# Softmax scaling of two heads in four moved from VectorE to GpSimd in a hybrid attention kernel

## The chip, the cores and the metric

The kernel runs on one core of a Trainium2 chip. The metric is device time in microseconds; lower is better. A difference is judged against the spread of the runs of the kernel before.

## What is computed

One layer of width 1024 on 512 tokens: a gated feed-forward block (inner width 2816), an attention mixer, a second feed-forward block and a final norm. In the mixer, eight heads use three branches side by side (compressed keys, selected blocks, and a window as long as the sequence) and eight heads use a window of 128 with a sink. For 512 tokens and eight blocks the selection takes all blocks, so the selected branch is plain causal attention. What matters here:

```python
s = jnp.where(mask, s + bias, NEG_INF)
p = jax.nn.softmax(s, axis=-1)
o = jnp.einsum('bngrqk,bnkgd->bnqgrd', p, vw)
...
g = jax.nn.sigmoid(gate_logits)
return g[..., 0:1] * o_cmp + g[..., 1:2] * o_slc + g[..., 2:3] * o_win
```

## The kernel before, in words

Everything is float32, and each large product is done as three matmuls of split halves (helper `mm3_steps`, L207 to L209: weight high by activation high, by activation low, weight low by activation high). The weight halves are made on the chip: ScalarE rounds (L97), VectorE subtracts (L98).

The mixer works in stages. A stage is one block of 128 queries (index i, 0 to 3), one group g of four heads, and one branch. There are eight stages of class `Swa` (the 128 window) and then fourteen of class `Nsa`: br 1 (selected) and br 2 (window, with the compressed branch beside it) for i = 1, 2, 3, and br 0 (both together) for i = 0. A row of probabilities is 128 or 256 wide in `Swa`, and 256, 384 or 512 wide in `Nsa` for i = 1, 2, 3.

`scores()` of a stage does for each of four heads r: the score matmuls (L838, L839) and the bias matmul (L918), a row maximum on VectorE (L911, in `Swa` L1037), an exponential on ScalarE with the row sum accumulated (L912, in `Swa` L1049). Then come the gate and the reciprocal (L973, L974; in `Swa` L1052, L1053), and each head's probabilities, a tile `tmp`, are multiplied in place by the resulting column of `su`: this is the line of the change, L985 with head 2 on ScalarE at L983, and L1055 in `Swa`. In stages of br 0, L979 does it, which the change doesn't touch.

`outputs()` of a stage then transposes the four heads' probabilities on TensorE, key block by key block (`transposed`, L847, four transposes into one PSUM bank, head 0 first), splits the result (ScalarE L849, VectorE L850) and multiplies by the values (L884, L885). `put_o` copies and splits the result (L855, L860, L866, L867).

`attend` lines the stages up: three heads of scores of a stage, then in turn a step of the outputs of the stage before and a head of scores. Between these steps it puts pieces of other work, the fillers, worked off in a fixed list: projections, the compression network, and the output projection (L1077 adds its result). The code writes down an order of the work; the order of instructions on each engine is made from it when the kernel is built. There is no DMA issued from GpSimd; all are on SP's queue.

Of the kernel before, what the change touches and what calls it, by code (L numbers as in the profile page):

```python
# [13 lines left out]
ALU = mybir.AluOpType  # L14
# [30 lines left out]
def tile_hybrid(ctx, tc, xT, f1_wi, f1_wo, wm_t, wm_n, cw1, cw2, small, wm_oa, wm_ob, wm_oc, f2_wi, f2_wo, const, out):  # L45
    nc = tc.nc
    V, A, PE = nc.vector, nc.scalar, nc.tensor
# [7 lines left out]
    def ps(tag="mm"):  # L55
        return psp.tile([P, 512], F32, tag=tag, name=tag, bufs=NB[tag])
# [17 lines left out]
    def tmp():  # L74
        return sb.tile([P, 512], F32, tag="tmp", name="tmp", bufs=NTMP)
# [563 lines left out]
    def slopes(g):  # L639
        if state["slopes"][0] == g:  # L640
            return state["slopes"][1]
        a = tabs[:, 512:1024].rearrange("p (r k) -> p r k", r=4)
        b = tabs2[:, 0:256].bitcast(BF16).rearrange("p (r k) -> p r k", r=4)
        for r in range(4):
            V.tensor_scalar(a[:, r, :], ident, 2.0 ** -(g * 4 + r + 1), None, op0=ALU.mult)
            V.tensor_scalar(b[:, r, :], ident, 2.0 ** -(g * 4 + r + 1), None, op0=ALU.mult)
        state["slopes"] = g, (a, b)
        return a, b
# [187 lines left out]
    def score(o, q, r, i, k1, k2):  # L836
        qs = slice(i * P, (i + 1) * P)
        PE.matmul(o, q[:, r % 2, qs], k1, start=True, stop=False)  # L838
        PE.matmul(o, q[:, r % 2, qs], k2, start=False, stop=False)  # L839

    def small_t(n, name):
        return sb.tile([P, n], F32, tag="st" + name, name=name, bufs=3)
# [46 lines left out]
    class Nsa:  # L889
# [5 lines left out]
        def scores(self):  # L895
# [5 lines left out]
            c0, c1 = ((0, 12), (0, 4), (4, 12))[br]  # L901
            nm, su = small_t(12, "nm"), small_t(12, "su")
# [25 lines left out]
            for r in range(4):  # L928
                q = Q[4 + 2 * g + r // 2]
                o = ps("sc")  # L930
                p = tmp()[:, : 2 * W if br == 0 else W]
# [43 lines left out]
            for r in range(4):  # L975
                p = self.p[r]
                if br == 0:
                    pv = p.rearrange("p (a b) -> p a b", a=2)
                    V.tensor_tensor(  # L979
                        pv, pv, su[:, r : r + 8 : 4].unsqueeze(2).to_broadcast([P, 2, P]), op=ALU.mult  # L980
                    )
                elif r == 2:
                    A.activation(p, p, AF.Copy, scale=su[:, c0 + r : c0 + r + 1])  # L983
                else:
                    V.tensor_scalar(p, p, su[:, c0 + r : c0 + r + 1], None, op0=ALU.mult)  # L985
            if br != 1:
# [25 lines left out]
    class Swa:  # L1012
# [5 lines left out]
        def scores(self):  # L1018
            g, i, W, c0 = self.g, self.i, self.W, self.c0
            sid, sidb = slopes(g)  # L1020
            nm, su, es = small_t(12, "nm"), small_t(12, "su"), small_t(4, "es")
            sink = nsink[:, g * 4 : g * 4 + 4]
            os_ = []
            for pr in range(2):
                bank = ps("sc")
                for rr in range(2):
                    r = pr * 2 + rr
                    o = bank[:, rr * 256 : rr * 256 + W]
                    score(o, Q[9 + 2 * g + pr], r, i, SK[0][:, g, c0 : c0 + W], SK[1][:, g, c0 : c0 + W])
                    if i == 0:  # L1030
                        PE.matmul(o, sidb[:, r, :], diag, start=False, stop=True)
                    else:
                        PE.matmul(o, sid[:, r, :], dist[:, 256:512], start=False, stop=False)
                        PE.matmul(o[:, :P], idb, swm, start=False, stop=True)
                    os_.append(o)
                    yield 0.4
                V.tensor_reduce(  # L1037
                    nm[:, pr * 2 : pr * 2 + 2], bank.rearrange("p (a b) -> p a b", a=2)[:, :, :W],
                    axis=AX.X, op=ALU.max, negate=True,
                )  # L1040
                if pr == 0:
                    V.tensor_tensor(nm[:, 0:2], nm[:, 0:2], sink[:, 0:2], op=ALU.min)
                else:
                    V.tensor_tensor(nm[:, 2:4], nm[:, 2:4], sink[:, 2:4], op=ALU.min)
            V.tensor_tensor(es, nm[:, :4], sink, op=ALU.subtract)
            self.p = []
            for r in range(4):
                a = tmp()[:, :W]
                A.activation(a, os_[r], AF.Exp, bias=nm[:, r : r + 1], accum_out=su[:, r : r + 1])  # L1049
                self.p.append(a)  # L1050
            A.activation(es, es, AF.Exp)
            V.tensor_tensor(su[:, :4], su[:, :4], es, op=ALU.add)  # L1052
            V.reciprocal(su[:, :4], su[:, :4])  # L1053
            for r in range(4):
                V.tensor_scalar(self.p[r], self.p[r], su[:, r : r + 1], None, op0=ALU.mult)  # L1055
            yield 0

        def outputs(self):
# [216 lines left out]
```

## Time and profile before

| | us |
|---|---|
| median of 3 runs | 1015.99 |
| lowest and highest run | 1015.99 and 1016.55 |
| the profiled execution, its own time | 1014.31 |
| its span, first to last instruction | 1012.5 |
| mean granted TensorE clock | 0.988 |

The profile shows one execution. The feed-forward block takes the span up to about 375 us, the mixer's projections reach to 410, the stages run from 410 to about 632, the mixer's last output projection ends near 700, and the second feed-forward block fills the rest. Lines are those of the kernel before; PE is TensorE's matmul, PEld its weight load, DVE VectorE, ACT ScalarE, POOL GpSimd.

### The profile page before, as it was taken

What the parts mean: (1) busy time and instruction counts of PE and PEld (TensorE: products, weight loads), DVE (VectorE), ACT (ScalarE), POOL (GpSimd) and SP (SyncE); (2) the same over time, 40 slices, a digit from 0 to 9 for tenths busy, and PEclk for the clock granted to TensorE, in tenths of its full rate; (3) what the DMA queues carried; (4) which work ended last, traced back from release to release, by engine and by line L of the source; (5) the groups of instructions that cost most, each with busy time, mean ns of one, the idle gap of its engine ahead of it and who ended that gap; (6) DMA issues with size and microseconds to landing.
All of it is one profiled execution on the core that took longest, in us unless ns stands there. A gap on an engine that the chain in (4) does not pass through costs nothing.

```text
span 1012.5 us, 15908 instructions
## 1 busy us (share of the span) xinstructions
PE 982.1 (97%) x6196; PEld 869.0 (86%) x6196; DVE 804.2 (79%) x1466; ACT 509.6 (50%) x1034; POOL 0.2 (0%) x4
## 2 busy tenths in 40 slices
PE   7799999999999999999999999989999999999997
PEld 5589999999999889788777777769999999999996
DVE  5889878788796675787889898788986878879665
ACT  7544434444344355554677675854434445344344
POOL 0000000000000000000000000000000000000000
PEclk9899999999999999999999999989999999999998
DMA  7053233222324303123311111115322323322112
GB/s 294 1 187 111 77 115 123 87 105 73 114 84 140 122 34 113 42 84 99 117 42 45 40 43 63 48 50 172 116 90 98 136 73 106 113 75 95 42 43 84
DMA packets 36508, 93.62 MB, mean 92 GB/s; under 512 B 4432, under 2 KB 8912, under 8 KB 36432
## 3 DMA queue, kind: packets, MB, share of 16 engines
q1 hardware_dynamic: 36432, 92.59, 26.8%
q8 instruction: 49, 0.80, 0.3%
q14 instruction: 27, 0.22, 0.1%
HBM read 88.87 MB, written 2.10 MB: 90 GB/s over the span
## 4 chain that ended last, share of the span: by engine, by line
PE 89%; DVE 6%; ACT 4%; issue 1%; DMA 1%; SPq 0%; DVEq 0%; ACTq 0%
PE mm L306 9%; PE mm L305 9%; PE mm L307 9%; PE sc L209 8%; PE sc L208 8%; PE sc L207 8%; PE mm L207 4%; PE mm L209 4%; PE mm L208 4%; PE sc L306 4%; PE sc L307 4%; PE sc L305 4%; PE mm L847 3%; PE pv L884 2%; PE pv L885 2%; PE mm L703 1%
## 5 line engine op out<-in xcount | busy, mean ns | idle before, releaser
L306 PE MATMUL mm<-u 128*128 128x256 f32 x760 | 214.5, 282 | 0.0
L307 PE MATMUL mm<-u 128*128 128x256 f32 x760 | 214.4, 283 | 0.0
L305 PE MATMUL mm<-u 128*128 128x256 f32 x760 | 214.3, 282 | 0.0
L207 PE MATMUL sc<-u 128*128 128x512 f32 (+1 forms) x400 | 156.5, 391 | 13.0 <-ACT u L97 12.0
L209 PE MATMUL sc<-u 128*128 128x512 f32 (+1 forms) x400 | 155.4, 388 | 0.8 <-DVE u L98 0.8
L208 PE MATMUL sc<-u 128*128 128x512 f32 (+1 forms) x400 | 155.8, 390 | 0.0
L305 PEld LDWEIGHTS mm<-u 128*128 128x128 f32 x760 | 144.5, 190 | 7.2 <-DVE tmp L512 0.5
L306 PEld LDWEIGHTS mm<-u 128*128 128x128 f32 x760 | 144.8, 191 | 5.6
L307 PEld LDWEIGHTS mm<-u 128*128 128x128 f32 x760 | 144.7, 191 | 0.6
L207 PE MATMUL mm<-u 128*128 128x512 f32 (+1 forms) x248 | 100.3, 404 | 4.6 <-ACT u L97 4.6
L209 PE MATMUL mm<-u 128*128 128x512 f32 (+1 forms) x248 | 96.6, 389 | 0.8 <-DVE u L98 0.8
L208 PE MATMUL mm<-u 128*128 128x512 f32 (+1 forms) x248 | 95.7, 386 | 0.6 <-DVE u L163 0.6
L207 PEld LDWEIGHTS sc<-u 128*128 128x128 f32 x400 | 77.3, 193 | 21.0 <-ACT u L97 12.9
L209 PEld LDWEIGHTS sc<-u 128*128 128x128 f32 x400 | 76.4, 191 | 20.4 <-DVE u L98 2.6
L307 PE MATMUL sc<-u 128*128 128x256 f32 x304 | 85.9, 283 | 0.0
L306 PE MATMUL sc<-u 128*128 128x256 f32 x304 | 85.9, 283 | 0.0
L305 PE MATMUL sc<-u 128*128 128x256 f32 x304 | 85.7, 282 | 0.0
L208 PEld LDWEIGHTS sc<-u 128*128 128x128 f32 x400 | 77.2, 193 | 6.5
L357 ACT CAST u<-tmp 128x512 fp32r<-128x512 f32 (+1 forms) x96 | 54.7, 583 | 45.4 <-PE sc L209 22.6
L380 DVE SCALAR_TENSOR_TENSOR h<-sc,h 128x512 f32<-128x512 f32 x85 | 58.3, 686 | 12.3 <-PE sc L209 12.3
L358 DVE TENSOR_TENSOR u<-tmp,u 128x512 fp32r<-128x512 f32 (+1 forms) x96 | 60.9, 640 | 8.9 <-ACT u L357 8.7
L493 ACT COPY mm<-sc 128x256 f32<-128x256 f32 x38 | 13.6, 357 | 94.7 <-PE sc L307 94.2
(221 smaller groups left out, 1994.4 us busy)
## 6 DMA issues: line engine op xcount, KB each, us to landing
t<-in_f_wi_dram SPq DMA_DIRECT2D x86, 512.0 KB, 4.4
tmp<-in_f_wo_dram SPq DMA_DIRECT2D x80, 256.0 KB, 4.7
t<-in_wm_t_dram SPq DMA_DIRECT2D x13, 512.0 KB, 4.4
t<-in_cw_dram SPq DMA_DIRECT2D x8, 512.0 KB, 4.9
tmp<-in_f_wo_dram SPq DMA_DIRECT2D x16, 128.0 KB, 4.0
t<-in_wm_oa_dram SPq DMA_DIRECT2D x4, 512.0 KB, 4.1
out_dram<-tmp SPq DMA_DIRECT2D x8, 256.0 KB, 2.1
t<-in_wm_n_dram SPq DMA_DIRECT2D x4, 408.0 KB, 3.7
```

Of the source, the lines that this page charges most:

```text
L207: PE.matmul(o, wh[:, c], xs[k][:, 0, :], start=s0, stop=False)
L208: PE.matmul(o, wh[:, c], xs[k][:, 1, :], start=False, stop=False)
L209: PE.matmul(o, wl[:, c], xs[k][:, 0, :], start=False, stop=s1)
L305: PE.matmul(o, w[0][:, c], x[k][0], start=new, stop=False, skip_group_check=not first)
L306: PE.matmul(o, w[0][:, c], x[k][1], start=False, stop=False, skip_group_check=not first)
L307: PE.matmul(o, w[1][:, c], x[k][0], start=False, stop=k == 3, skip_group_check=not first)
L357: A.copy(u[:, 0, :n], raw[:, :n])
L358: V.tensor_tensor(u[:, 1, :n], raw[:, :n], f(u[:, 0, :n]), op=ALU.subtract)
L380: V.scalar_tensor_tensor(h[:, i, :], o, 0.5, h[:, i, :], op0=ALU.mult, op1=ALU.add)
L847: PE.transpose(pt[:rows, r * P : (r + 1) * P], pl[r][:, cols], ident)
L884: PE.matmul(pv, v, u[:rows, 0, :], start=a, stop=False)
L885: PE.matmul(pv, v, u[:rows, 1, :], start=False, stop=b)
```

## The change

Heads 0 and 3 of the twelve `Nsa` stages of br 1 and br 2, and heads 0 and 2 of the eight `Swa` stages, are scaled by GpSimd; heads 1 (and 3 in `Swa`) stay on VectorE, head 2 in `Nsa` on ScalarE.

```diff
@@ -981,6 +981,8 @@
                     )
                 elif r == 2:
                     A.activation(p, p, AF.Copy, scale=su[:, c0 + r : c0 + r + 1])
+                elif r in (0, 3):
+                    nc.gpsimd.tensor_scalar(p, p, su[:, c0 + r : c0 + r + 1], None, op0=ALU.mult)
                 else:
                     V.tensor_scalar(p, p, su[:, c0 + r : c0 + r + 1], None, op0=ALU.mult)
             if br != 1:
@@ -1052,7 +1054,8 @@
             V.tensor_tensor(su[:, :4], su[:, :4], es, op=ALU.add)
             V.reciprocal(su[:, :4], su[:, :4])
             for r in range(4):
-                V.tensor_scalar(self.p[r], self.p[r], su[:, r : r + 1], None, op0=ALU.mult)
+                E = nc.gpsimd if r in (0, 2) else V
+                E.tensor_scalar(self.p[r], self.p[r], su[:, r : r + 1], None, op0=ALU.mult)
             yield 0
```

## Rows read from the trace of the kernel before

**Rows 1.** The page, part 1: busy us, share of the span, instructions.

```profile
PE 982.1 (97%) x6196; PEld 869.0 (86%) x6196; DVE 804.2 (79%) x1466; ACT 509.6 (50%) x1034; POOL 0.2 (0%) x4
```

**Rows 2.** The page, part 4: the chain that ended last, by engine.

```profile
PE 89%; DVE 6%; ACT 4%; issue 1%; DMA 1%; SPq 0%; DVEq 0%; ACTq 0%
```

**Rows 3.** Busy time by stretch: PE, PEld, DVE, ACT, POOL, PE clock, DMA.

```profile
410.00:490.00 80.00, 78.97 (x482) 66.16 (x481) 66.22 (x188) 41.54 (x124) 0.00 (x0) 1.00 0.27 82
490.00:632.00 142.00, 139.83 (x784) 108.25 (x783) 123.35 (x305) 99.84 (x300) 0.00 (x0) 1.00 0.15 49
```

**Rows 4.** Waits, 410 to 632 us: us in total, times, longest.

```profile
PEld pv L885 <- DVE u L850: 2.0, 6, 0.7
PEld sc L838 <- ACT u L912: 1.9, 4, 0.9
PEld sc L838 <- ACT tmp L912: 1.7, 2, 1.1
```

**Rows 5.** Groups: busy us, mean ns; the ScalarE line with minimum, median, maximum ns.

```profile
L985 DVE TENSOR_SCALAR tmp<-tmp,su 128x256 f32<-128x256 f32 (+2 forms) x36 | 12.8, 409 | 0.0
L1055 DVE TENSOR_SCALAR tmp<-tmp,su 128x256 f32<-128x256 f32 (+1 forms) x32 | 8.6, 327 | 0.1
L983 ACT ACTIVATE tmp<-tmp,su x12: 501/612/724, 509.5 to 615.7; 128x256 f32<-128x256 f32 x4, 128x384 f32<-128x384 f32 x4, 128x512 f32<-128x512 f32 x4
```

**Rows 6.** Groups: GpSimd's widest kind, and VectorE's subtraction of weights.

```profile
L1261 POOL MEMSET const-float32-1.0<- 128x1 f32 x1 | 0.1, 98 | 0.0
L98 DVE TENSOR_TENSOR u<-t,u 128x1024 fp32r<-128x1024 f32 x31 | 37.8, 1221 | 9.8 <-ACT u L97 9.6
```

**Rows 7.** Timeline, 384-wide stage (group 0, i 2, br 1): start, us, what.

```profile
526.53 1.07 DVE L985 TENSOR_SCALAR tmp<-tmp,su 128x384 f32<-128x384 f32 x3
527.52 0.84 DVE L860 TENSOR_TENSOR tmp<-pv,tmp 64x256 f32<-64x256 f32 x2
...
526.12 0.61 ACT L983 ACTIVATE tmp<-tmp,su 128x384 f32<-128x384 f32 x1
...
527.80 0.20 ACT L912 ACTIVATION_READ_ACCUMULATOR tmp<-sc,nm 128x1 f32 x1
528.39 0.50 ACT L866 CAST u<-tmp 128x128 fp32r<-128x128 f32 x2 [0.39 <-DVE tmp L860]
...
527.09 1.50 PE L847 MATMUL mm<-ident,tmp 128*128 128x128 f32 x12
529.22 0.46 PE L838 MATMUL sc<-t,u 128*128 128x416 f32 x1 [0.62 <-ACT u L912]
```

**Rows 8.** Timeline, last 512-wide stage (group 1, i 3, br 2).

```profile
616.10 1.27 DVE L985 TENSOR_SCALAR tmp<-tmp,su 128x512 f32<-128x512 f32 x3
...
615.72 0.72 ACT L983 ACTIVATE tmp<-tmp,su 128x512 f32<-128x512 f32 x1 [0.93 <-DVE su L974]
...
616.72 1.83 PE L847 MATMUL mm<-ident,tmp 128*128 128x128 f32 x13 [0.20 <-DVE tmp L985]
```

**Rows 9.** Timeline, 256-wide stage (group 0, i 1, br 2).

```profile
518.25 0.51 ACT L983 ACTIVATE tmp<-tmp,su 128x256 f32<-128x256 f32 x1
...
518.94 0.86 PE L847 MATMUL mm<-ident,tmp 128*128 128x128 f32 x5
```

**Rows 10.** Timeline, 512-wide stage (group 0, i 3, br 2).

```profile
555.67 0.72 ACT L983 ACTIVATE tmp<-tmp,su 128x512 f32<-128x512 f32 x1 [1.57 <-DVE su L974]
...
556.81 0.38 PE L847 MATMUL mm<-ident,tmp 128*128 128x128 f32 x2
556.95 0.48 PE L209 MATMUL mm<-u 128*128 128x512 f32 x1
557.27 0.60 PE L847 MATMUL mm<-ident,tmp 128*128 128x128 f32 x4
```

**Rows 11.** Timeline, a 256-wide Swa stage (group 1, i 2).

```profile
432.30 1.14 DVE L1055 TENSOR_SCALAR tmp<-tmp,su 128x256 f32<-128x256 f32 x4
...
435.29 0.60 PE L847 MATMUL mm<-ident,tmp 128*128 128x128 f32 x4
```

## The prediction

> **What bounds the kernel now.** I read the page's engine line first: TensorE is busy for 97% of the span, VectorE for 79%, and GpSimd does nothing [rows 1]. The chain that ended last says the same: 89% of it is TensorE, 6% VectorE [rows 2]. A share over the whole span is a mean over two feed-forward blocks and a mixer, so I went to the stretches in which the changed lines run. In 410 to 490 us (Swa stages) TensorE is busy 78.97 of 80 us and in 490 to 632 us (Nsa stages) 139.83 of 142 us, at full granted clock; VectorE is busy 66.22 and 123.35 us there [rows 3]. So TensorE is the bound in both, VectorE is a crowded second (123.35 / 142 = 87%), and the idle time that TensorE shows is only 1.03 + 2.17 = 3.2 us. VectorE's time counts only where TensorE waits for it. The table of waits names where that is: weight loads wait 2.0 us for VectorE's split of the transposed probabilities, and 1.9 + 1.7 us for exponentials on ScalarE (L912), which free a PSUM bank for the next scores [rows 4]. These are short waits, 12 in all.
>
> Last I took the timeline around each scaling, to see how long a scaled tile lies before its first transpose. That distance, and not the load of VectorE, decides what a slower engine costs.
>
> **What is removed.** 24 of the 36 operations of L985 and 16 of the 32 of L1055 leave VectorE: 12.8 x 24/36 = 8.5 us and 8.6 x 16/32 = 4.3 us [rows 5], 12.8 us together. This is the ceiling of the gain if all of it lay on the path. It does not. I find it on the path at two places. At 526.5 three scalings keep VectorE for 1.07 us; the two operations of L860 stand behind them, then ScalarE's L866, then an exponential, and a score matmul at 529.22 waits 0.62 us for that [rows 7]. With one scaling left, L860 comes two thirds of the distance from 526.53 to 527.52 earlier, 0.66 us. ScalarE is busy until 528.00 (527.80 + 0.20), so L866 can start 0.39 us earlier, not 0.66: a gain of **0.4 us**. At 616.1 the transposes wait 0.20 us for the first scaling, which VectorE could begin only at 616.10, while ScalarE, released by the same reciprocal, began its head at 615.72 [rows 8]. GpSimd has an empty queue and can begin with ScalarE: a gain of **0.2 us**. Together 0.6 us.
>
> **What is added.** 40 operations on GpSimd, two in a row in each of 20 stages, with a wait for VectorE's reciprocal before the first, and a wait of the transposes for GpSimd. No row shows GpSimd on a wide tile; there is only a memset of one column, 98 ns [rows 6]. I bound the price of a 512-wide scaling. Below: VectorE's own L985, whose group of three takes 1.27 us [rows 8], 0.42 us apiece. Above: half the rate of VectorE's two-operand subtraction, that is 1024 columns' time for 512, 1.22 us [rows 6]; for narrower tiles in proportion 0.92 and 0.61 us. I take ScalarE's time for the same operation on the same tile, 0.72, 0.61 and 0.50 us for 512, 384 and 256 columns [rows 5], since it is the row nearest in kind: another engine that reads and writes one element per lane and has to be woken by VectorE.
>
> What lies beside other work: the second GpSimd operation has to be done before the third (Swa) or fourth (Nsa) transpose, which comes about 0.22 or 0.33 us after the first (two in a row take 0.38 us and four 0.60, so each adds 0.11) [rows 10]. The start is that of ScalarE's L983, which waits for the same reciprocal. By these rules the four closest stages have, from the start to the transpose of head 3:
> - 256 wide: 518.94 + 0.33 - 518.25 = 1.02 us [rows 9], needed 2 x 0.50 = 1.00;
> - 384 wide: 527.09 + 0.33 - 526.12 = 1.30 us [rows 7], needed 1.22;
> - 512 wide, group 0: 557.38 - 555.67 = 1.71 us (fourth transpose, 0.11 after 557.27) [rows 10], needed 1.44;
> - 512 wide, group 1: 616.72 + 0.33 - 615.72 = 1.33 us [rows 8], needed 1.44, so 0.11 us late.
>
> The other eight Nsa stages have more room than these. In Swa the tiles lie long: VectorE finishes at 433.44 (432.30 + 1.14) and the first transpose is at 435.29, 1.85 us later [rows 11]; two GpSimd operations of 0.50 us begun with VectorE's first end at 433.30, ahead of that. One of the eight is close but fits at this price. So Swa costs nothing, covered by the filler matmuls between; if those were gone, it would still end where VectorE ends now. Waking GpSimd may take a little more than waking ScalarE; I put 0.05 us for each of the four stages, an estimate, 0.2 us. **Added: 0.1 + 0.2 = 0.3 us.**
>
> Behind GpSimd's waits nothing is queued, since it has no other work and issues no DMA; no DMA is moved. `su` and the `tmp` tiles are held no longer than a transpose lasts.
>
> **Sum.** -0.6 + 0.3 = **-0.3 us** on the profiled execution's 1014.31 us. The median of the runs is 1.68 us above that execution, and I carry the difference: 1015.99 - 0.3 = **1015.7 us**.
>
> A rule bears on the price. No run here shows it, and the sum stands without it: the Trainium skill, page "GPSIMD Engine Reference", section "Elementwise — side-by-side cycle accounting", has 1.8 cycles an element as the best case of a tight loop there and 769 ns for 512 elements; by an estimate from that page two 512-wide operations would take 1.54 us and the last stage would be 0.2 us late instead of 0.1.
>
> **Rivals.**
>
> *Faster: VectorE's relief goes further than two places.* For it: VectorE is 87% busy in the Nsa stretch, so every operation stands behind others there, and L911's maxima, which ScalarE's exponentials need, will come earlier by up to two scalings, 0.71 to 0.85 us a wide stage (two thirds of 1.07 and 1.27, [rows 7, 8]). Against it: TensorE shows little idle time. If all waits of [rows 4] went, that is 5.6 us; I take 3.5 us as the likely size of this case, since part of those weight loads is already covered by running matmuls: 1012.5 us.
>
> *Slower: GpSimd and VectorE hold each other up over the tiles.* Place: the same four stages. Price at the upper bound: 2 x 0.61 - 1.02 = 0.20, 2 x 0.92 - 1.30 = 0.54, 2 x 1.22 - 1.71 = 0.73, 2 x 1.22 - 1.33 = 1.11, in all 2.6 us late; less the 0.6 us gained, 1018.0. If besides VectorE's remaining head has to go between the two GpSimd operations, because both can't work on SBUF at once, each stage is later by that head, 0.36 and 0.42 us for 384 and 512 columns (a third of 1.07 and 1.27), by width some 0.25 for 256, in all 0.25 + 0.36 + 2 x 0.42 = 1.45 us: 1019.5 us. It decides from about 0.65 us for 384 and 512 columns, where two operations no longer fit 1.3 us. For it: no row shows the two engines at work together. Against it: ScalarE and VectorE scale heads at the same time at present [rows 7, 8], and the price that I take fits.
>
> The Trainium skill, page "SBUF — State Buffer", section "Who interferes with whom", says that a VectorE scaling that uses both its ports and a GpSimd operation exclude each other, the later one waiting for the whole of the first; no row here can show that, as GpSimd is idle. By that rule the case with turns is the likelier half of this rival.
>
> *The order changes.* The code issues four transposes in one loop, yet the trace has a filler matmul (L209) between the second and the third [rows 10]: the build reorders instructions. Other engines for 40 operations may give another order on TensorE in all of the mixer, for better or worse, by several waits of the size seen (0.2 to 0.6 us, [rows 7, 8]), some 2 to 3 us either way: 1013 or 1018.5 us.
>
> That the change does not do what it says can be excluded but for size: stages of br 0 keep L979, so the 40 are of the 68 of L985 and L1055.
>
> **How the numbers follow.** A difference within 0.2%, 2.0 us, is about what a measurement of this kernel can't tell from none. Chances: my forecast 0.39, relief 0.27, GpSimd too slow or in the way 0.21, another order 0.13, of which a little under half each way. Faster by over 2 us: 0.27 + 0.05 = 0.32. Slower: 0.21 + 0.06 = 0.27. Within: 0.41. The range goes down to 1011.0, somewhat below the relief case (its ceiling is 1010.4), and up to 1020.0, just above the case with turns. The likeliest case alone spans 1014 to 1017.5.
>
> **What would show it.** If I am right: GpSimd operations of about 0.5 to 0.75 us; VectorE's busy time down by some 12 us; the score matmul near 529 waiting less than 0.3 us; TensorE's waits for the scaled tiles (L847 behind GpSimd) under 0.5 us in sum. It is wrong towards slower if L847 waits for GpSimd by 2 us or more, or VectorE's remaining L985 grows beyond 0.5 us or starts late; towards faster if TensorE's busy time in 490 to 632 packs into a stretch shorter by 2 us or more.

## The result and the profile after

The changed kernel takes 1023.97 us (median of 4 runs, 1023.0 to 1025.81) against 1015.99: a ratio of 1.008 with a 95% interval of 1.0065 to 1.0095. Run again beside the second set of experiments it came out at 1.0078 (1.0066 to 1.0091). The forecast was 1015.7 us with a range up to 1020.0; the change costs 8 us and lies outside. The profiled execution is the slowest of the four, 1025.81 us with a span of 1022.7, so its span is read for where the time sits and the medians for how much it is.

The page's engine line and its chain by engine, which answer to [rows 1] and [rows 2]:

```profile
PE 986.0 (96%) x6196; PEld 870.5 (85%) x6196; DVE 797.6 (78%) x1426; ACT 510.6 (50%) x1034; POOL 49.3 (5%) x44
PE 82%; DVE 8%; ACT 5%; POOL 2%; issue 1%; DMA 1%; POOLq 0%; SPq 0%; DVEq 0%; ACTq 0%
```

GpSimd is busy for 49 us; the price I took gives about 23 (16 operations of Swa and 8 of each Nsa width). VectorE's busy time falls by only 6.6 us, not 12.8. GpSimd now stands in the chain.

The stretches of [rows 3], in the same columns:

```profile
410.00:490.00 80.00, 77.75 (x470) 66.32 (x470) 62.27 (x169) 41.18 (x123) 13.42 (x16) 0.98 0.27 82
490.00:632.00 142.00, 134.93 (x749) 102.30 (x748) 112.17 (x272) 97.32 (x294) 35.68 (x25) 0.99 0.14 45
```

TensorE is idle for 142 - 134.93 = 7.1 us of the Nsa stretch; before, it was 2.2. The waits of TensorE from 410 to 632 us, which answer to [rows 4], name the releaser:

```profile
PEld mm L847 <- POOL tmp L985: 10.7, 13, 1.7
PE mm L847 <- POOL tmp L985: 6.5, 10, 1.2
PEld sc L838 <- ACT u L912: 1.9, 6, 0.7
PEld mm L847 <- POOL tmp L1058: 1.5, 2, 0.8
PE mm L847 <- POOL tmp L1058: 0.7, 2, 0.4
PEld sc L838 <- ACT tmp L912: 0.9, 3, 0.4
```

The transposes wait for GpSimd's tiles. A weight load and its matmul wait side by side, so the rows of PEld and PE are not to be added; the matmuls' rows, 6.5 + 0.7 = 7.2 us, are the time that TensorE stands behind GpSimd. The weight loads' waits for L912 shrink only from 1.9 + 1.7 us to 1.9 + 0.9. Where TensorE stands is seen in its timeline, here from the first group's stages at i = 1, 2 and 3:

```profile
521.77 0.44 PE L847 MATMUL mm<-ident,tmp 128*128 128x128 f32 x2 [1.17 <-POOL tmp L985]
...
523.59 1.10 PE L847 MATMUL mm<-ident,tmp 128*128 128x128 f32 x4 [0.70 <-POOL tmp L985]
...
534.06 0.98 PE L847 MATMUL mm<-ident,tmp 128*128 128x128 f32 x7 [1.08 <-POOL tmp L985]
535.40 0.76 PE L847 MATMUL mm<-ident,tmp 128*128 128x128 f32 x5 [0.36 <-POOL tmp L985]
...
563.24 1.04 PE L847 MATMUL mm<-ident,tmp 128*128 128x128 f32 x8
```

Lines 985 and 987 are the GpSimd and VectorE scaling of Nsa in the changed kernel, 1058 both of them in Swa. Their groups, which answer to [rows 5]:

```profile
L985 POOL TENSOR_SCALAR tmp<-tmp,su 128x512 f32<-128x512 f32 x8 | 13.8, 1733 | 26.8 <-DVE su L974 23.8 <-PE mm L847 3.0
L985 POOL TENSOR_SCALAR tmp<-tmp,su 128x384 f32<-128x384 f32 x8 | 10.4, 1316 | 25.4 <-PE sc L918 17.9 <-ACT tmp L912 5.3 <-PE mm L209 2.2
L985 POOL TENSOR_SCALAR tmp<-tmp,su 128x256 f32<-128x256 f32 x8 | 9.9, 1248 | 49.7 <-DVE su L974 34.6 <-ACT u L97 15.1
L987 DVE TENSOR_SCALAR tmp<-tmp,su 128x512 f32<-128x512 f32 x4 | 2.6, 642 | 0.0
```

This is the number that decides the case: 1.73 us for 512 columns, where I took 0.72 and gave 1.22 as the highest. Undisturbed it is somewhat less. The timeline of the last stage, which answers to [rows 8], has the two operations in 3.10 us, 1.55 apiece:

```profile
624.55 3.10 POOL L985 TENSOR_SCALAR tmp<-tmp,su 128x512 f32<-128x512 f32 x2 [11.52 <-DVE su L974]
...
624.84 0.68 DVE L987 TENSOR_SCALAR tmp<-tmp,su 128x512 f32<-128x512 f32 x1
...
624.53 0.40 PE L209 MATMUL mm<-u 128*128 128x512 f32 x1
626.17 0.33 PE L847 MATMUL mm<-ident,tmp 128*128 128x128 f32 x1 [1.24 <-POOL tmp L985]
...
627.71 0.66 PE L847 MATMUL mm<-ident,tmp 128*128 128x128 f32 x4 [0.42 <-POOL tmp L985]
```

GpSimd does begin as soon as the reciprocal is there, as predicted, 0.1 us behind ScalarE's L983 at 624.46 where I had put 0.05. Head 0 is ready at 626.1 and the first transpose follows at once, after 1.24 us of idle TensorE; head 3 is ready at 627.7 and releases four more transposes, after another 0.42 us.

### The profile page after: what moved, and what is told of

Read it like the earlier page. It is cut to its first block, busy times and chain, and to the rows that moved or that the text cites. A ratio compares the mean times of both kernels' runs of the same rounds, so it can differ in the third digit from the quotient of the medians.

```text
span 1022.7 us, 15998 instructions
## 1 busy us (share of the span) xinstructions
PE 986.0 (96%) x6196; PEld 870.5 (85%) x6196; DVE 797.6 (78%) x1426; ACT 510.6 (50%) x1034; POOL 49.3 (5%) x44
## 4 chain that ended last, share of the span: by engine, by line
PE 82%; DVE 8%; ACT 5%; POOL 2%; issue 1%; DMA 1%; POOLq 0%; SPq 0%; DVEq 0%; ACTq 0%
PE mm L306 9%; PE mm L305 9%; PE mm L307 9%; PE sc L209 8%; PE sc L208 8%; PE sc L207 8%; PE sc L306 4%; PE sc L307 4%; PE sc L305 3%; PE mm L207 3%; PE mm L209 3%; PE mm L208 3%; PE mm L847 2%; POOL tmp L985 2%; PE pv L884 1%
```

## The experiments

The theory to test is **waiting**: GpSimd is slow, its second tile comes later than TensorE wants it, and TensorE stands. The rivals are **the lock** (GpSimd and VectorE hinder each other in SBUF, whoever waits for the result) and **the order** (the build moved 496 of 6204 TensorE instructions). All were timed against the kernel before on the same chip, in three sets.

### The two parts alone

```diff
 # Nsa part only: the change, with Swa put back
-                E = nc.gpsimd if r in (0, 2) else V
-                E.tensor_scalar(self.p[r], self.p[r], su[:, r : r + 1], None, op0=ALU.mult)
+                V.tensor_scalar(self.p[r], self.p[r], su[:, r : r + 1], None, op0=ALU.mult)
 # Swa part only: the change, with Nsa put back
-                elif r in (0, 3):
-                    nc.gpsimd.tensor_scalar(p, p, su[:, c0 + r : c0 + r + 1], None, op0=ALU.mult)
```

> Only the Nsa part of the change; Swa is scaled by VectorE as before. The trace after shows a GpSimd scaling that nothing holds up at 0.92, 1.24 and 1.56 us for 256, 384 and 512 columns, two in a row, against 1.02 to 1.9 us of room in the close stages. Waiting theory (TensorE waits for GpSimd's second tile): +6 to +7 us against before, nearly all of the +8. Lock theory (GpSimd and VectorE exclude each other in SBUF, and each operation costs alike): 24 of 40 operations, about +5. Order theory (the build puts TensorE's instructions in another order): by the share of moved instructions about +6.

> Only the Swa part of the change. Waiting theory: the room in Swa is 1 to 3 us beyond VectorE's end in seven of eight stages, so 0 to +1.5 us. Lock theory: 16 of 40 operations, about +3. Order theory: by the share of moved instructions on TensorE (157 against 496) about +2.5.

The Nsa part alone takes 1021.3 us, ratio 1.005 (1.0037 to 1.0062), +5.4 us. Waiting had said +6 to +7, the lock +5 and the order +6, so this run decides nothing. The Swa part alone takes 1016.75 us, ratio 1.0003 (0.9994 to 1.0012): no difference that the runs can tell, where the lock said +3 and the order +2.5. Sixteen of the forty operations cost next to nothing, where the tiles lie long enough. That speaks against a fixed toll for each operation, and against a loss in proportion to moved instructions, and fits waiting.

### GpSimd at work, nobody waiting

```diff
 # the change, with the product written to a spare tile
-                    nc.gpsimd.tensor_scalar(p, p, su[:, c0 + r : c0 + r + 1], None, op0=ALU.mult)
+                    nc.gpsimd.tensor_scalar(scr[:, :W], p, su[:, c0 + r : c0 + r + 1], None, op0=ALU.mult)
...
-                E.tensor_scalar(self.p[r], self.p[r], su[:, r : r + 1], None, op0=ALU.mult)
+                E.tensor_scalar(scr[:, :W] if r in (0, 2) else self.p[r], self.p[r], su[:, r : r + 1], None, op0=ALU.mult)
```

> GpSimd reads the same tiles at the same places, but writes its product to a spare tile, and the transposes take heads 0 and 3 (0 and 2 in Swa) unscaled: VectorE is relieved and GpSimd is as busy as in the change, but TensorE does not wait for it. TensorE's order is nearly that of the changed kernel (117 of 6204 instructions differ). Waiting theory: the loss goes, 1013 to 1016.5 us (before, less up to 3 us of relief). Order theory: stays at 1022 to 1024. Lock theory: stays above 1020.

It takes 1013.68 us, ratio 0.9978 (0.9967 to 0.9989): 2.2 us faster than before. It leaves out the scaling of the two heads in the values that follow; the instructions and GpSimd's load are those of the change, and the order is nearly its own. So the order and GpSimd's mere presence don't make the loss; the wait does. Between this kernel and the change lie 1.0078 - 0.9978, or 1.0%: waiting for GpSimd costs **about 10 us**, set against **2.2 us of relief**. Of the 10, the trace after has 7.2 as idle time of TensorE behind GpSimd; the rest is not located. The mean granted clock, 0.991 in this profile and 0.988 before, is not what gains: from the mixer's first matmul (L799) to the long wait behind its stages the two profiles take 288.6 us before (376.35 to 664.99) and 286.5 here (377.66 to 664.16), both at full clock until that wait. The relief's stretches:

```profile
410.00:490.00 80.00, 79.53 (x494) 67.64 (x493) 65.53 (x174) 42.15 (x124) 15.38 (x16) 1.00 0.29 87
490.00:632.00 142.00, 141.05 (x783) 108.97 (x782) 118.40 (x283) 101.60 (x302) 33.25 (x24) 1.00 0.15 49
```

TensorE's idle time goes from 1.03 + 2.17 us [rows 3] to 0.47 + 0.95, 1.8 us less. Not all of it is VectorE's relief: the transposes here wait for no scaling of heads 0 and 3, and the 0.20 us at 616.72 [rows 8] go by that alone. The score matmul that waited 0.62 us at 529.22 [rows 7] still waits, first line; another one's wait, second line, of the kernel before, is gone, third line:

```profile
528.70 0.46 PE L838 MATMUL sc<-t,u 128*128 128x416 f32 x1 [0.51 <-ACT u L912]
...
539.55 0.28 PE L838 MATMUL sc<-t,u 128*128 128x32 f32 x1 [0.68 <-ACT tmp L912]
...
538.31 0.18 PE L838 MATMUL sc<-t,u 128*128 128x32 f32 x1
```

### GpSimd's load beside the kernel before

```diff
 # the kernel before, with GpSimd scaling a spare tile beside VectorE
-                    V.tensor_scalar(p, p, su[:, c0 + r : c0 + r + 1], None, op0=ALU.mult)
+                    V.tensor_scalar(p, p, su[:, c0 + r : c0 + r + 1], None, op0=ALU.mult); r != 1 and nc.gpsimd.tensor_scalar(scr[:, :W], scr[:, :W], su[:, c0 + r : c0 + r + 1], None, op0=ALU.mult)
...
-                V.tensor_scalar(self.p[r], self.p[r], su[:, r : r + 1], None, op0=ALU.mult)
+                V.tensor_scalar(self.p[r], self.p[r], su[:, r : r + 1], None, op0=ALU.mult); r in (0, 2) and nc.gpsimd.tensor_scalar(scr[:, :W], scr[:, :W], su[:, r : r + 1], None, op0=ALU.mult)
```

> The kernel before, with the same order of instructions on TensorE, VectorE and ScalarE, and 40 GpSimd scalings of a spare tile added at the places of the change: VectorE does all its work, GpSimd runs beside it, and nothing waits for GpSimd. Waiting and order theory: the time of before, within 1 us. Lock theory: +4 to +8 us, and VectorE's two-input subtractions and scalings visibly longer.

It takes 1019.49 us, ratio 1.003 (1.0019 to 1.0042). The instructions of TensorE, VectorE and ScalarE stand in the order of before, and nothing waits for GpSimd, so these 3.6 us between the medians (3.0 by the ratio) are contention. Waiting alone expected none of it: the two engines do hinder each other, by a little less than the lock theory said. Whether they meet in SBUF no run shows. Which operations grew is seen in the groups, first two of this kernel:

```profile
L985 DVE TENSOR_SCALAR tmp<-tmp,su 128x384 f32<-128x384 f32 x12 | 7.2, 650 | 0.0
L985 DVE TENSOR_SCALAR tmp<-tmp,su 128x512 f32<-128x512 f32 x12 | 7.1, 646 | 0.0
L867 DVE TENSOR_TENSOR u<-tmp,u 128x128 fp32r<-128x128 f32 x32 | 7.9, 282 | 0.0
```

and then the same two of the kernel before:

```profile
L985 DVE TENSOR_SCALAR tmp<-tmp,su 128x384 f32<-128x384 f32 x12 | 4.3, 408 | 0.0
L985 DVE TENSOR_SCALAR tmp<-tmp,su 128x512 f32<-128x512 f32 x12 | 5.1, 478 | 0.0
```

VectorE's scalings of these widths grow from 0.41 and 0.48 us to 0.65, the longest to 0.84; its subtraction L867 with two inputs takes 283 ns before and 282 here, against the lock theory. How a scaling grows is to be seen in one stage of the loaded kernel:

```profile
545.20 3.73 POOL L985 TENSOR_SCALAR scr<-scr,su 128x512 f32<-128x512 f32 x2 [7.10 <-DVE su L974]
...
545.51 1.98 DVE L985 TENSOR_SCALAR tmp<-tmp,su 128x512 f32<-128x512 f32 x3
```

Three scalings take 1.98 us instead of 1.27 [rows 8] and are done at 547.49, while GpSimd works without a break from 545.20 to 548.93.

### One head instead of two

```diff
 # Swa put back, and in Nsa
-                elif r in (0, 3):
+                elif r == 3:      # the other kernel: r == 0
```

> In the twelve Nsa stages only head 3 goes to GpSimd, head 0 stays on VectorE; Swa as before. Waiting theory: one operation of 0.92, 1.24 or 1.56 us has to be done by the transpose of head 3, and the close stages leave 1.02, 1.30, 1.71 and 1.33 us, so only the last is late, by 0.2 us; against that stands about a third to a half of VectorE's relief: -1.5 to +0.5 us against before. If the loss goes with the number of GpSimd operations (12 of 24) or with the order (375 moved instructions on TensorE against 374 in the run with heads 0 and 3): +2.5 to +5 us.

> The same with head 0 alone on GpSimd and head 3 on VectorE. Waiting theory: head 0's transpose comes first, 0.33 us sooner than head 3's, so the same operation is late by 0.2, 0.3, 0.4 and 0.6 us in the four close stages, some 1.5 us: 0 to +1.5 us against before, and 1 to 1.5 us slower than head 3 alone. By count of operations it would be equal to head 3 alone.

Head 3 alone: 1016.35 us, ratio 1.0008 (0.9999 to 1.0017). Head 0 alone: 1017.98 us, 1.0024 (1.0014 to 1.0033). The same number of the same operations differs by 1.6 us, by when the tile is needed; waiting expected 1 to 1.5. Both came out above the range that it gave: +0.7 where at most +0.5 was expected, and +2.3 where at most +1.5. I had set a share of the relief against the waits; that this share is missing with one head is argued, not shown. The waits for GpSimd, head 3 alone (only weight loads) and then head 0 alone:

```profile
PEld mm L847 <- POOL tmp L985: 0.6, 2, 0.3
```

```profile
PEld mm L847 <- POOL tmp L985: 5.1, 7, 1.4
PE mm L847 <- POOL tmp L985: 2.3, 4, 1.0
```

### More room for the same work

```diff
 # the change, with the first block of heads 0 and 3 left to VectorE
                 elif r in (0, 3):
-                    nc.gpsimd.tensor_scalar(p, p, su[:, c0 + r : c0 + r + 1], None, op0=ALU.mult)
+                    V.tensor_scalar(p[:, :P], p[:, :P], su[:, c0 + r : c0 + r + 1], None, op0=ALU.mult)
+                    nc.gpsimd.tensor_scalar(p[:, P:], p[:, P:], su[:, c0 + r : c0 + r + 1], None, op0=ALU.mult)
 # the change, and the kernel before as its control, with outputs begun a step later
-            for _ in range(3):
+            for _ in range(4):
                 step(sc, share)
```

> The change, but in the twelve Nsa stages VectorE scales the first 128 columns of heads 0 and 3, which are transposed first, and GpSimd only the columns behind them (128, 256 or 384: about 0.60, 0.92, 1.24 us by the trace after). Waiting theory: each GpSimd piece is 0.3 us shorter and is needed a block of transposes and values later, a microsecond or more, so most of the +5.4 of the Nsa part goes: +0.5 to +3 us against before. If the number of GpSimd operations or the order made the loss: +7 to +8 as in the change (VectorE has 24 small operations more).

> The change, with the outputs of a stage begun after four instead of three steps of the next stage's scores, so that every transpose has one step (three or four matmuls and a filler) more room. Waiting theory: a step is 0.5 to 1 us, most waits for GpSimd shrink, and it comes out 3 to 8 us faster than the change (1016 to 1021). Otherwise it stays at 1022 to 1025.

> The control for the run before: the kernel before with the same four steps, VectorE scaling everything. VectorE's tiles were late nowhere by more than 0.2 us, so it should gain nothing: 1014 to 1018 us. If it is slower, the step itself costs that much and the other run is to be read against it.

The later blocks: 1016.9 us, ratio 1.0015 (1.0006 to 1.0024). With 24 GpSimd operations in Nsa as in the change, and the Swa part as well, the loss goes from 7.8 to 1.5 us. Outputs a step later: 1020.0 us, 1.0045 (1.0032 to 1.0058); its control 1017.13 us, 1.0012 (1.0003 to 1.0021). Against the control the change costs 0.33%, 3.4 us, instead of 7.8. So both ways of giving room work. In the traces TensorE's idle time behind GpSimd, 7.2 us in the change, is 0.9 us in Nsa and 0.7 in Swa with the later blocks, and 2.9 us with the outputs a step later, so the loss goes with it. None of these versions is faster than the kernel before.

### The change again, and another use of GpSimd

> The changed kernel once more, on the same chip as the other runs of this set, since its parts alone gave +5.4 and +0.3 us and the whole +8. If the parts add up, 1021 to 1022 us here; if the two parts act on each other, 1023 to 1025 us again.

It took 1023.29 us, ratio 1.0078 (1.0066 to 1.0091). The parts, 5.4 and 0.3, don't add up to it; some 2 us are theirs together, not much more than the intervals of the three ratios leave open. The profile shows two things that the change has and the Nsa part alone has not. One is more waiting, TensorE's for GpSimd in the Nsa part alone:

```profile
PE mm L847 <- POOL tmp L985: 4.2, 8, 1.0
```

In the change it is 6.5 us, and 0.7 for Swa. The 2.3 us more lie mostly in two stages. In that of [rows 9] the two GpSimd operations take 3.14 us (from 520.39), VectorE's subtraction of weights L98 running beside the second, and 2.68 in the Nsa part alone; TensorE waits 1.17 + 0.70 us instead of 0.71 + 0.29. In that of [rows 7] its matmuls wait 1.08 + 0.36 us, and not at all in the Nsa part alone. The other thing is the clock. TensorE around 522 us in this run (stage of [rows 9]):

```profile
520.72 0.40 PE L209 MATMUL mm<-u 128*128 128x512 f32 x1
522.26 0.44 PE L847 MATMUL mm<-ident,tmp 128*128 128x128 f32 x2 [1.15 <-POOL tmp L985]
...
524.09 0.84 PE L847 MATMUL mm<-ident,tmp 128*128 128x128 f32 x4 [0.70 <-POOL tmp L985]
...
526.86 0.63 PE L208 MATMUL mm<-u 128*128 128x512 f32 x1
527.29 0.63 PE L209 MATMUL mm<-u 128*128 128x512 f32 x1
```

and the stretches around it in the same columns as above:

```profile
515.00:520.00 5.00, 5.00 (x29) 4.08 (x27) 4.02 (x13) 4.83 (x20) 0.00 (x0) 1.00 0.00 0
520.00:524.00 4.00, 2.24 (x12) 1.37 (x10) 3.90 (x8) 1.65 (x3) 3.11 (x2) 1.00 0.02 4
524.00:527.50 3.50, 3.41 (x13) 2.68 (x14) 1.93 (x4) 2.35 (x6) 0.03 (x1) 0.56 0.91 293
```

TensorE is busy 2.24 of 4 us, having waited twice for GpSimd, and in the next 3.5 us its granted clock is 0.56: it runs mostly at 1.2 instead of 2.4 GHz, and large matmuls start 0.43 us apart (526.86, 527.29) instead of 0.23 (562.78, 563.01 in the first profile of the change, at full clock). At nearly half speed, 3.5 us of work lose about 1.5. The first profile of the change has the same fall in this stage and one more in the Swa stretch (0.98 above); that of the Nsa part alone has a mean clock of 1.00 from 490 to 640 us. So in these two executions the wait is paid a second time. But they have mean clocks of 0.988 and 0.986, and those that set the two medians have 0.991, as the profiled execution of the Nsa part alone has without the fall; 3.5 us at 0.56 would lower the mean by 0.0015. So the fall is probably not in the medians, and the longer waits fit the 2 us better. No run tells the two apart.

```diff
 # the kernel before, with the late subtraction of put_o on GpSimd
-            V.tensor_tensor(u[:, 1, ts], ob[:, a, :], f(u[:, 0, ts]), op=ALU.subtract)
+            nc.gpsimd.tensor_tensor(u[:, 1, ts], ob[:, a, :], f(u[:, 0, ts]), op=ALU.subtract)
```

> The change undone; instead VectorE is relieved of work that nobody waits for soon: the 32 subtractions L867 (128x128, two inputs, 0.28 us each, 7.9 us in all), whose result the output projection reads much later, go to GpSimd. If relief of VectorE is worth something once TensorE does not wait for GpSimd: -1 to -3 us against before. If GpSimd's work beside VectorE's scalings takes as much as it gives: within 1 us.

This was meant as a version to beat both. It took 1018.92 us, ratio 1.0027 (1.0016 to 1.0039): slower, against both halves of the expectation, though no wait of TensorE or VectorE for GpSimd shows. Its profile has TensorE at a clock of 0.57 with 10 matmuls in 486 to 489.5 us, where that of the changed kernel run beside it has 17 at 1.00; 7 matmuls at 0.23 us would be 1.6 of the 2.7 us. Its six runs all have a mean clock of 0.989, as the profiled one; whether all had this fall, and what made the rest, stays open.

## Why the prediction was wrong

**What bounds the kernel** held: TensorE, with VectorE on the path at few places. Reading the distance from the reciprocal to the transposes instead of VectorE's load was the right view. Three of the four close stages have 5.0 of TensorE's 7.2 us behind GpSimd: 1.17 + 0.70, 1.08 + 0.36 and 1.24 + 0.42. The fourth, 512 wide in group 0, has none, since TensorE comes to its transposes only at 563.24, when both tiles are done (562.79); the rest lies in the eight stages said to have more room, and 0.7 us in Swa.

**The step that failed is the price of the added operation.** The text took 0.72, 0.61 and 0.50 us, ScalarE's times, and bounded it above at 1.22 us for 512 columns. Undisturbed, the trace after has 1.55 us for 512, and the shortest 256-wide one takes 0.92. The upper bound was no bound: "half the rate of VectorE's two-operand subtraction" is a row of another engine with a factor that I chose, and nothing in the trace before limited GpSimd. With 1.55 us, and 0.92 for 256 and 1.24 for 384 between them, the working of the text itself gives 2 x 0.92 - 1.02 = 0.82, 2 x 1.24 - 1.30 = 1.18, 2 x 1.55 - 1.71 = 1.39 and 2 x 1.55 - 1.33 = 1.77, in all **5.2 us late**; less 0.6 it would have forecast +4.6 and a slower kernel. Stage by stage the waits were 1.87, 1.44, 0 and 1.66 us: the method holds in the last; in the first two GpSimd was also slowed (3.14 and 2.90 us for the pair instead of 1.84 and 2.48); in the third TensorE's order now has other work first. The 0.1 us late of the sum's +0.3 was thus some 5 to 7 us. The text's own signs of a slower kernel both came: waits at L847 of 6.5 us where it named 2, and VectorE's remaining scaling of 512 columns at 0.64 us where it named 0.5. The sign hung on this one price, and its decision point (0.65 us) stood in the text. The sentence on the Trainium skill, page "GPSIMD Engine Reference", section "Elementwise — side-by-side cycle accounting", gave 769 ns for 512 elements; the measured 1.55 us is twice that, so the trace does not agree with this estimate for a scaling by a column.

**The relief** was 0.6 us in the sum, and the kernel in which nobody waits gains 2.2 us, contention included. The relief rival's 3.5 us was too much. And the 0.6 was not right in its parts. Of the 0.4 us that I put at 529 the kernel in which nobody waits has 0.1 (a wait of 0.51 instead of 0.62 us), and it gains at 539.55 instead, 0.68 us that I had not found. In the change itself the score matmul in that place (536.24) doesn't wait; TensorE has just stood 1.08 + 0.36 us for GpSimd, so this shows no gain.

**The slower rival** had the right mechanism, TensorE waiting for GpSimd's tiles, and three of its four places, and too low a price. Its second half, VectorE's head going between two GpSimd operations, is not what happens: at 624.84 its scaling starts while GpSimd's first is under way. The rule of the Trainium skill, page "SBUF — State Buffer", section "Who interferes with whom", that the later of the two is blocked for the whole instruction, does not agree with the loaded kernel: beside GpSimd operations of 1.6 us and more a VectorE scaling takes 0.65 us on average in place of 0.48. It is held up, but by 0.17, and by 0.36 at most.

**The order** as a cause by itself falls: with nearly the same order and no wait the kernel is faster than before.

**Swa costs nothing** held in the time, 1.0003, and not quite in the reason: at 0.92 us apiece one stage no longer fits, and TensorE waits 0.7 us in it, alone as in the change (L1058 above).

## What to carry to other kernels

Moving work from a crowded engine to an idle one pays only where its result lies unused for longer than the idle engine needs; measure the distance from the input's release to the first reader in the trace, stage by stage, and add up what is missing. The order that the build makes may move that reader, as in one of the four stages here. When the new engine's price isn't in the trace, the sign of the forecast may hang on it: then either get it measured first, or give the case beyond your bound its chance. A stall of a busy TensorE may be paid twice, once as idle time and once as a lower clock behind it, as in both profiles of the change.

## What the runs showed of the hardware that was not expected

A scaling by a column on GpSimd, undisturbed, costs 0.92 us for 256 columns and 1.55 for 512, 2.5 ns a column and some 0.3 us besides; VectorE takes 0.42 apiece for 512 in a row, ScalarE 0.72. The two-input subtraction of 128 columns in the last experiment took GpSimd 0.52 us on average.

GpSimd and VectorE hinder each other unequally. In the loaded kernel VectorE's scaling of 512 columns grows from 0.48 to 0.65 us, its two-input subtraction L867 does not. GpSimd, though, takes 0.9 to 1.1 us longer in the four operations of the changed kernel beside which most of VectorE's long two-input subtraction of weights runs. In the changed kernel's 512-wide stage of [rows 10] the pair takes 4.04 us instead of 3.10:

```profile
558.75 4.04 POOL L985 TENSOR_SCALAR tmp<-tmp,su 128x512 f32<-128x512 f32 x2 [5.92 <-DVE su L974]
...
559.85 1.21 DVE L98 TENSOR_TENSOR u<-t,u 128x1024 fp32r<-128x1024 f32 x1
```

The subtraction keeps its 1.21 us [rows 6].
